# Two layers of a diffusion backbone on one core: latent tiles' norms placed behind the MLP's last squares, their transposes amid a projection, and a gate's store moved

## The chip, the cores and the metric

The kernel runs on one core of a Trainium2 chip. The time is device microseconds of one execution. An execution under the profiler gives the trace; its times count from the start of the span, which is the stretch between the first and the last instruction on the engines. In the rows, PE is the matrix engine (TensorE; PEld are its weight loads), DVE is VectorE, ACT is ScalarE, POOL is GpSimd and SP is the engine that issues DMAs (SPq its queue of issues).

## The reference, cut to what matters

512 latent tokens and 256 context tokens of 1024 channels go through two layers. Layer 0 mixes tokens by pooling, layer 1 by attention. Each sub-layer is normed before and after, modulated by vectors of a condition, and gated into a residual.

```python
for i in range(DEPTH):
    sh1, sc1, gt1, sh2, sc2, gt2 = ada_mods(c, w_ada[i], b_ada[i])
    h_lat = modulate(rms_norm(x, g_mix_pre[i]), sh1, sc1)
    h_ctx = modulate(rms_norm(ctx, g_mix_pre[i]), csh1, csc1)
    ...
    y_lat, y_ctx = attention_mixer(h_lat, h_ctx, w_qkv[j], g_q[j], g_k[j], w_o[j], not last)
    x = x + gt1 * rms_norm(y_lat, g_mix_post[i])
    m_lat = sq_relu_mlp(modulate(rms_norm(x, g_mlp_pre[i]), sh2, sc2), w_mlp_in[i], w_mlp_out[i])
    x = x + gt2 * rms_norm(m_lat, g_mlp_post[i])
```

## The kernel before

Tokens are handled in tiles of 128: tiles 0 to 3 are the latents, 4 and 5 the context. Every fp32 operand of a matmul is split into an upper and a lower part (hi and lo), and each product is three matmuls, so a projection of one tile by 512 columns is 24 matmuls (8 blocks of channels, three products each).

A scheduler, run when the program is built, orders each engine's instructions by its own estimate of time; the steps that the kernel records (`st.at(time, step, ...)`) give it their order of priority. `pin` and `tc.add_manual_dep(..., ISSUE)` fix the order of two instructions on one engine without a semaphore. What an engine then executes is a fixed list, each entry waiting for its semaphores; an entry that waits holds up all behind it on its engine.

The change touches two places.

The first is the passage from layer 0's MLP to layer 1's attention. `finish` takes the six tiles in the order 4, 5, 0, 1, 2, 3. For each it makes the last MLP product (`out_mm`: 24 matmuls into two banks called pso; for four of the tiles ACT first copies the earlier partial sum into the bank, a seed). Behind it come the steps of `last0` for this tile: `norm_a` squares the two halves on ACT (`junk<-pso`) and makes the post-norm's factor (its power is on POOL, `rs`), `norm_g` multiplies the sums by the gate on DVE (`work<-pso,gate`), which frees the banks, `norm_r` adds the result to the residual (`xl`, `xr`), `norm_s` squares the new residual on ACT (`junk<-xl`) for layer 1's norm, and `norm_c` scales the residual into `acc`. Two tiles together are then turned (`norm_pair`: 16 PE transposes into two psx buffers, eight modulations that ACT and DVE share, and the split into hi and lo parts, `ra`). At last `kv_a` projects one tile to keys and values (`project`, 24 matmuls into a psq bank), `kv_e`, `kv_b` and `kv_c` take the result on. Four banks (pool psB) serve pso, psq and pk in turn, and two double banks (psA) serve psx. The weights of the projection are split between the engines at the same time: three of the four lower parts of the second half are made on POOL (`units<-raw,units`).

The second place is the gate of attention's residual. It is 1024 numbers, made on DVE as a column of eight for each partition (`gate_cols`, tile gc), stored by a DMA to `grows` in DRAM (`gate_away`, issued on SP) and loaded back as one row for all partitions (`gate_back`). In the kernel before, `before0` calls `gate_away(1, GT1, 0)`, and the scheduler puts its product and its store in the midst of layer 0's MLP, amid loads of MLP weights that SP issues in order. The readers of the gate are the output steps of attention (`attn_ev`).

Of the kernel before, what the change touches and what calls it, by code (L numbers as in the profile page):

```python
# [17 lines left out]
P = 128  # L18
# [22 lines left out]
class Steps:  # L41
# [3 lines left out]
    def at(self, t, fn, *args):  # L45
        self.items.append((t, len(self.items), fn, args))
# [7 lines left out]
def backbone(ctx: ExitStack, tc, x, c, ctx_in, c_ctx, w_ada, b_ada, g_mix_pre, g_mix_post,  # L54
# [306 lines left out]
                      parts.rearrange("p (u c b a) -> p a u b c", c=nc_, b=2, a=4)[:, a], start=True, stop=True)  # L361
        ada_out(i, m, 0, ps[:, 0:2 * n], nc_, 8)

    def gate_cols(i, m, ci):
        gc = sm_tile("gc")
        g0 = (0 if m == GT1 else 16) + i * KT
        z = ve.tensor_tensor(out=gc, in0=mods[i][:, m * KT:(m + 1) * KT, ci], in1=gpc[:, g0:g0 + KT],
                         op=ALU.mult)
        pin(z, (i, m) == (0, GT1))
        if (i, m) == (1, GT2):  # L370
            tc.keep_in_program_order(z)
        return gc

    def gate_rows(i, m, ci):
# [8 lines left out]

    row_of = {(0, GT2, 0): 0, (0, GT2, 1): 1, (1, GT1, 0): 2, (1, GT2, 0): 3}

    def gate_away(i, m, ci):
        gc = gate_cols(i, m, ci)
        with nc.allow_non_contiguous_dma(reason="one column of gates for each partition"):
            sy.dma_start(rows_out[row_of[i, m, ci]].rearrange("(k p) -> p k", p=P), gc)

    def gate_back(i, m, ci):
        sy.dma_start(gate[:, ci, :], rows_out[row_of[i, m, ci]].partition_broadcast(P))

    def gate_half(h):
        gc = sm_tile("gc")
# [28 lines left out]
    def modulated_pair(t, i, s, hi, lo, works, wide, fine, on_act):  # L424
        if (i, s) == (0, 1):
            place = lambda z, ks: z.rearrange("p k (h q n) -> p k q h n", h=2, n=P)[:, ks, t // 2]
            split2 = lambda z: z.rearrange("p k (h n) -> p k h n", n=P)
        else:
            place, split2 = lambda z, ks: z[:, ks, slice(t * P, (t + 2) * P)], lambda z: z
        ci = 0 if t < NL else 1  # L430
        sh = (SH1, SH2)[s] * KT
        pss = []
        for q in range(4):
            if not wide:
                ps = psB.tile([P, 2, 256], F32, tag="b", name="psx")
            elif q % 2 == 0:
                both = psA.tile([P, 4, 256], F32, tag="a", name="psx")
            if wide:
                ps = both[:, 2 * (q % 2):2 * (q % 2) + 2, :]
            for kk in range(2):  # L440
                k = 2 * q + kk
                for u in range(2):
                    turned_[t] = te.transpose(ps[:, kk, u * P:(u + 1) * P], works[u][:, k * P:(k + 1) * P], ident)
            pss.append(ps)
        for q in range(4):
            h = works[q // 2][:, 512 * (q % 2):512 * (q % 2) + 512].rearrange("p (k n) -> p k n", n=256)
            for kk in range(2):
                k = 2 * q + kk
                sa, b = avec[i][s][:, k, ci:ci + 1], mods[i][:, sh + k, ci:ci + 1]
                if not on_act[k]:  # L450
                    ve.tensor_scalar(out=h[:, kk, :], in0=pss[q][:, kk, :], scalar1=sa, scalar2=b,
                                     op0=ALU.mult, op1=ALU.add)
                else:
                    sc.activation(h[:, kk, :], pss[q][:, kk, :], AF.Identity, scale=sa, bias=b)
            if fine:
                ks = slice(2 * q, 2 * q + 2)
                sc.copy(place(hi, ks), split2(h))
                ve.tensor_tensor(out=place(lo, ks), in0=split2(h), in1=place(hi, ks), op=ALU.subtract)
            elif q % 2:
                ks = slice(2 * q - 2, 2 * q + 2)  # L460
                h = works[q // 2].rearrange("p (k n) -> p k n", n=256)
                sc.copy(place(hi, ks), split2(h))
                if (i, s, q) == (1, 1, 3):
                    late.extend((place(lo, z), h[:, z.start - 4:z.stop - 4], place(hi, z)) for z in (slice(4, 6), slice(6, 8)))
                else:
                    ve.tensor_tensor(out=place(lo, ks), in0=split2(h), in1=place(hi, ks), op=ALU.subtract)
# [841 lines left out]

    b3 = lambda a: a.rearrange("p (h d) -> p h d", d=HD)

    def project(t, ws):
        ps = psB.tile([P, 512], F32, tag="b", name="psq")
        sl = slice(t * P, (t + 1) * P)
        for k in range(KT):
            wH, wL = ws[k // 4]
            for n, (a, w) in enumerate(((hH, wH), (hH, wL), (hL, wH))):
                te.matmul(ps, a[:, k, sl], w[:, k % 4, :], start=(k == 0 and n == 0),
                          stop=(k == KT - 1 and n == 2))
        return ps

    exps = {}
# [38 lines left out]
    pj = {}  # L1360
# [16 lines left out]
            gated(t, yg[t], src, c0, c0 + w, pool)  # L1377

    def kv_a(t):
        pj[t] = project(t, chunks[2])  # L1380

    def kv_e(t):
        ps = pj[t]
# [36 lines left out]
    def last0(st, n, t):  # L1420
        st.at([5.25, 10.45, 15.65, 20.85, 26.05, 27][n], norm_a, t)
        st.at([5.473, 10.6, 15.8, 21, 26.2, 27.1][n], norm_g, t, (False, False, False, False, False, False)[n])
        st.at([8.8, 14, 19.2, 24.4, 28.4, 30.3][n], norm_r, t, (False, True, False, False, False, False)[n])
        st.at([10, 16.738, 20.4, 25.6, 28.5, 30.4][n], norm_s, t, (False, False, False, False, True, False)[n])
        st.at([12, 17.906, 22.4, 27.6, 30.2, 30.6][n], norm_c, t, (True, True, True, True, True, False)[n], (False, False, False, False, False, False)[n])
        if t < NL:
            st.at([0, 0, 22.5, 27.7, 33, 37][n], lambda t: sy.dma_start(spill[:, t], xr[:, t]), t)
        if n % 2:
            st.at([18.2, 28.6, 39][n // 2], norm_pair, t - 1, 1, 0, hH, hL, True, (True, True, False)[n // 2],
                  ((True, False, False, False, False, False, False, True), (True, True, True, False, False, False, True, True), (True, False, True, False, True, False, True, False))[n // 2])  # L1430
        st.at([31.4, 36.6, 41.8, 47, 55, 60.2][n], kv_a, t)
        st.at([36.874, 40.793, 45.993, 51.193, 59.193, 65.4][n], kv_e, t)
        st.at([36.9, 42.1, 47.3, 52.5, 60.5, 65.7][n], kv_b, t)
        st.at([44.9, 50.1, 57.151, 62.351, 70.351, 75.551][n], kv_c, t)
        if t < NL:
            for ch in range(2):
                c = t + 4 * ch
                st.at([67.851, 73.051, 78.251, 81.6, 86.8, 92, 97.2, 104.478][c], q_a, ch, t)
                if c == 2 * NL - 1:
                    st.at(107.6, q_rest, ch, t)  # L1440
                st.at([71.2, 76.4, 81.6, 86.8, 92, 97.2, 102.4, 132][c], q_e, ch, t)
                st.at([71.5, 76.7, 81.9, 87.1, 92.3, 97.5, 102.7, 132.1][c], q_b, ch, t)
        if n == 5:
            st.at(18.4, rope_load)
            st.at(38.5, rope_tables)
            st.at(5.5, lambda: split(*raw0[0], True, False, True))
            raws = []
            st.at(31.3, w_chunk, 2, 1, raws)
            st.at(31.3, lambda: split(*raws[0], False, False, True, 0))
            st.at(31.301, lambda: split(*raws[0], False, False, True, 1))  # L1450
            st.at(31.302, lambda: split(*raws[0], False, False, True, 2))
            st.at(31.303, lambda: split(*raws[0], False, True, False, 3))
            st.at(52, w_chunk, 0, 0, raws)
            st.at(52.01, lambda: split(*raws[1], True, False, False))
            st.at(61, w_chunk, 0, 1, raws)
            st.at(61.01, lambda: split(*raws[2], True, False, False))
            st.at(61.1, w_chunk, 1, 0, raws)
            st.at(61.11, lambda: split(*raws[3], True, False, False))
            st.at(83, w_chunk, 1, 1, raws)
            st.at(83.01, lambda: split(*raws[4], True, False, False))  # L1460
            attention(st, 102.5, 2.7)
            output(st, 102.5 + 2.7 * 43.691)

    def before0():
        nonlocal xr, gate, junk
        for u in due:
            ada_fin(*u[1:])
        gate_away(1, GT1, 0)
        small.tile([P, 2, KT], F32R, tag="gh", name="phase2", bufs=2)
        S["held"].close()  # L1470
        xr, gate, junk = residents(held[1])
        gate_back(0, GT2, 1)
        gate_back(0, GT2, 0)
        for t in (4, 5, 0, 1, 2, 3):
            sy.dma_start(xr[:, t], spill[:, t])
        qring.append(Ring([unit[0], unit[2], unit[1]]))
        w_chunk(2, 0, raw0)
# [132 lines left out]
    def attention(st, base, unit_t):  # L1610
# [25 lines left out]
        at(39.192, lambda: split(*raws[3], False, False, False, 1))  # L1636
        at(39.193, lambda: split(*raws[3], False, False, False, 2))
        at(45.691, lambda: split(*raws[3], False, False, False, 3))
        at(36.95, gate_back, 1, GT1, 0)

    def output(st, base):
        at = lambda i, fn, *args: st.at(base + i, fn, *args)
# [95 lines left out]
```

## Time and profile before

| what | value |
|---|---|
| median of the runs | 1154.8 us (1154.6 to 1156.63, 3 runs) |
| the profiled execution itself | 1153.73 us |
| its span | 1151.9 us |
| mean granted clock of PE | 0.999 |
| loads of MLP input weights | 32, of 1 MB each |

Two ways to read the trace serve here. A timeline gives rows of "start, duration, engine, line, operation, output<-inputs, count", where a number in brackets is the idle time of the engine just before the row, and who ended it; equal instructions that follow each other are one row. A table of stretches gives, for each, the busy time of PE, PEld, DVE, ACT and POOL (with counts of instructions), the granted clock, the mean busy share of the DMA engines and the GB/s that they moved. Nearly all instructions have line 68, that of a helper, so rows are told apart by their tiles.

### The profile page before, as it was taken

To read this page: it belongs to the slowest core of one execution; us is meant where nothing else is said; L and a number is where in the kernel's file an instruction comes from. 1 tells how busy PE (TensorE), PEld (TensorE's weight loads), DVE (VectorE), ACT (ScalarE), POOL (GpSimd) and SP (SyncE) were. 2 spreads that over 40 slices of the span, in tenths; PEclk is the share of its full clock that TensorE was granted. 3 is DMA by queue.
4 is the path that set the end of the run, shared out by engine and by line. 5 is a ranking of instruction groups with operands and counts; after the bars stand their busy time and mean duration, and the time that the engine had idled before them with its cause. 6 is when DMAs were issued, how large, how long until landed. Compare 5 with 4: busy or idle time off the path is not lost.

```text
span 1151.9 us, 15610 instructions
## 1 busy us (share of the span) xinstructions
PE 1129.6 (98%) x5998; PEld 975.8 (85%) x5998; DVE 925.5 (80%) x1539; ACT 641.0 (56%) x1142; POOL 75.3 (7%) x82
## 2 busy tenths in 40 slices
PE   6999999999999999999999999999999999999998
PEld 5579889998888888989878889988988888888886
DVE  5798488889979999897577689977887779778875
ACT  6476655554335534555795468863876436435534
POOL 3040000000000000000241212100000000000000
PEclk9999999999999999999999999999999999999999
DMA  9992233244434434444652200046244224224303
GB/s 352 400 390 104 74 110 110 83 137 147 147 110 147 146 120 145 138 135 144 228 171 93 90 1 19 10 144 221 84 146 147 77 70 146 78 69 147 110 16 149
DMA packets 100042, 154.20 MB, mean 134 GB/s; under 512 B 7120, under 2 KB 72448, under 8 KB 99968
## 3 DMA queue, kind: packets, MB, share of 16 engines
q1 hardware_dynamic: 99872, 153.19, 38.5%
q8 instruction: 47, 0.77, 0.3%
q14 instruction: 27, 0.22, 0.1%
q10 hardware_dynamic: 96, 0.02, 0.0%
HBM read 143.75 MB, written 9.45 MB: 133 GB/s over the span
## 4 chain that ended last, share of the span: by engine, by line
PE 85%; ACT 5%; DVE 5%; DMA 3%; issue 1%; SPq 0%; POOL 0%; DVEq 0%; ACTq 0%
PE psin L68 32%; PE pso L68 30%; PE psq L68 7%; PE psy L68 4%; PE po L68 3%; PE pss L68 3%; DMA raw<-in_w_mlp_in 2%; PE pspt L68 1%; PE psada L68 1%; ACT junk L68 1%; PE pspool L68 1%; DVE acc L68 1%; DVE rows L68 1%; PE psx L68 1%; DMA raw<-in_w_ada 1%; ACT ra L68 1%
## 5 line engine op out<-in xcount | busy, mean ns | idle before, releaser
L68 PE MATMUL pso<-units,rb 128*128 128x512 f32 x1152 | 278.0, 392 | 0.0
L68 PEld LDWEIGHTS pso<-units,rb 128*128 128x128 f32 x1152 | 214.7, 188 | 42.0 <-ACT pso L68 0.7
L68 DVE TENSOR_TENSOR acc<-acc,pso 128x512 f32<-128x512 f32 x192 | 128.2, 681 | 62.2 <-PE pso L68 62.1
L68 DVE SCALAR_TENSOR_TENSOR rows<-raw,cond,rows 128x256 f32<-128x256 f32 x280 | 121.9, 478 | 0.9
L68 PE MATMUL psin<-ra 128*128 128x512 f32 (+1 forms) x424 | 112.3, 369 | 0.6 <-ACT work L68 0.6
L68 PE MATMUL psin<-ra,rb 128*128 128x512 f32 (+1 forms) x384 | 101.6, 360 | 0.1
L68 DVE TENSOR_TENSOR units<-raw,units 128x1024 fp32r<-128x1024 f32 (+2 forms) x69 | 82.9, 1212 | 16.2 <-ACT units L68 15.3
L68 ACT CAST units<-raw 128x1024 fp32r<-128x1024 f32 (+2 forms) x71 | 70.9, 1020 | 43.2 <-PE pso L68 19.6
L68 PE MATMUL psin<-rb,ra 128*128 128x384 f32 (+1 forms) x324 | 90.6, 356 | 0.0
L68 PEld LDWEIGHTS psin<-ra 128*128 128x128 f32 x424 | 77.9, 188 | 12.1 <-ACT work L68 1.0
L68 PE MATMUL psin<-ra,units 128*128 128x384 f32 x432 | 82.6, 336 | 0.0
L68 PE MATMUL pso<-units,pairs 128*128 128x512 f32 x336 | 82.3, 389 | 0.0
L68 ACT ACTIVATE work<-psin 128x512 f32<-128x512 f32 (+3 forms) x66 | 36.1, 552 | 82.0 <-PE psin L68 79.6
L68 PEld LDWEIGHTS psin<-ra,units 128*128 128x128 f32 x432 | 76.5, 188 | 2.8
L68 PEld LDWEIGHTS psin<-ra,rb 128*128 128x128 f32 x384 | 66.7, 189 | 11.6 <-issue 0.9
L68 PEld LDWEIGHTS pso<-units,pairs 128*128 128x128 f32 x336 | 63.1, 188 | 13.1
L68 PE MATMUL psin<-sums,units 128*128 128x384 f32 x336 | 63.9, 337 | 0.8 <-ACT psin L68 0.8
L68 PEld LDWEIGHTS psin<-rb,ra 128*128 128x128 f32 x324 | 58.6, 188 | 5.5
L68 PEld LDWEIGHTS psin<-sums,units 128*128 128x128 f32 x336 | 59.0, 188 | 2.4 <-ACT psin L68 1.2
L68 ACT COPY acc<-pso 128x512 f32<-128x512 f32 x68 | 38.5, 592 | 40.1 <-PE pso L68 39.9
L68 ACT ACTIVATE work<-work 128x768 f32<-128x768 f32 (+1 forms) x50 | 41.4, 831 | 32.2 <-DVE work L68 31.7
L68 ACT CAST rb<-raw 128x2048 fp32r<-128x2048 f32 (+2 forms) x18 | 25.8, 1432 | 58.9 <-PE pso L68 55.9
(221 smaller groups left out, 2093.1 us busy)
## 6 DMA issues: line engine op xcount, KB each, us to landing
raw<-in_w_ada SPq DMA_DIRECT2D x48, 1024.0 KB, 5.5
raw<-in_w_mlp_in SPq DMA_DIRECT2D x32, 1024.0 KB, 5.3
raw<-in_w_mlp_out SPq DMA_DIRECT2D x32, 1024.0 KB, 5.7
raw<-in_w_qkv SPq DMA_DIRECT2D x6, 1024.0 KB, 5.1
spill<-xl SPq DMA_DIRECT2D x8, 512.0 KB, 8.9
xl<-spill SPq DMA_DIRECT2D x8, 512.0 KB, 10.4
raw<-in_w_o SPq DMA_DIRECT2D x4, 1024.0 KB, 5.1
xl<-in_x SPq DMA_DIRECT2D x4, 512.0 KB, 5.6
```

The costliest lines, as they stand in the source:

```text
L68: z = made(*args, **kw)
```

## The change

Three edits, and what they do to each engine's list.

1. In `last0`, the steps `norm_s` and `norm_c` of the third and fourth tile (n = 2 and 3, which are latent tiles 0 and 1) get later times: 20.4 and 25.6 become 26.1 and 26.2, and `norm_c` of tile 0 goes from 22.4 to 26.15.
2. `kv_a` of context tile 5 gives `project` an instruction to stand behind: its matmuls for channel blocks 4 to 7 follow the last transpose of the pair of latent tiles 0 and 1.
3. `gate_away(1, GT1, 0)` moves from `before0` to a step of attention (time 3.3), with its product behind DVE's last modulation of latent pair 0; `gate_back(1, GT1, 0)` stands behind the copy of attention's ninth turn (`turned[8]`).

```diff
+        if behind is not None:
+            tc.add_manual_dep(z.ins, behind.ins.name, ISSUE, reason="row order")
         return gc
...
-    def gate_away(i, m, ci):
-        gc = gate_cols(i, m, ci)
+    def gate_away(i, m, ci, behind=None):
+        gc = gate_cols(i, m, ci, behind)
...
-    def gate_back(i, m, ci):
-        sy.dma_start(gate[:, ci, :], rows_out[row_of[i, m, ci]].partition_broadcast(P))
+    def gate_back(i, m, ci, behind=None):
+        z = sy.dma_start(gate[:, ci, :], rows_out[row_of[i, m, ci]].partition_broadcast(P))
+        if behind is not None:
+            tc.add_manual_dep(z.ins, behind.ins.name, ISSUE, reason="row order")
...
-                    ve.tensor_scalar(out=h[:, kk, :], in0=pss[q][:, kk, :], scalar1=sa, scalar2=b,
-                                     op0=ALU.mult, op1=ALU.add)
+                    turned_[t, ve] = ve.tensor_scalar(out=h[:, kk, :], in0=pss[q][:, kk, :], scalar1=sa, scalar2=b,
+                                                      op0=ALU.mult, op1=ALU.add)
...
-    def project(t, ws):
+    def project(t, ws, behind=None):
...
-                te.matmul(ps, a[:, k, sl], w[:, k % 4, :], start=(k == 0 and n == 0),
+                z = te.matmul(ps, a[:, k, sl], w[:, k % 4, :], start=(k == 0 and n == 0),
                           stop=(k == KT - 1 and n == 2))
+                if behind and k >= 4:
+                    tc.add_manual_dep(z.ins, behind.ins.name, ISSUE, reason="row order")
...
-        pj[t] = project(t, chunks[2])
+        pj[t] = project(t, chunks[2], turned_[0] if t == NL + 1 else None)
...
-        st.at([10, 16.738, 20.4, 25.6, 28.5, 30.4][n], norm_s, t, (False, False, False, False, True, False)[n])
-        st.at([12, 17.906, 22.4, 27.6, 30.2, 30.6][n], norm_c, t, (True, True, True, True, True, False)[n], (False, False, False, False, False, False)[n])
+        st.at([10, 16.738, 26.1, 26.2, 28.5, 30.4][n], norm_s, t, (False, False, False, False, True, False)[n])
+        st.at([12, 17.906, 26.15, 27.6, 30.2, 30.6][n], norm_c, t, (True, True, True, True, True, False)[n], (False, False, False, False, False, False)[n])
...
-        gate_away(1, GT1, 0)
...
-        at(36.95, gate_back, 1, GT1, 0)
+        at(3.3, lambda: gate_away(1, GT1, 0, turned_[0, ve]))
+        at(36.95, lambda: gate_back(1, GT1, 0, turned[8]))
```

On PE, from the turn of the context pair to the projections of latent tiles (pso are the last MLP products, psx the turns, psq the projections):

```order
 L68 MATMUL psx<-ident,acc 128x128 x14
 L68 MATMUL pso<-units,rb 128x512 x32
-L68 MATMUL psx<-ident,acc 128x128 x2
+L68 MATMUL psq<-rb,ra 128x512 x19
+L68 MATMUL psq<-units,ra 128x512 x4
+L68 MATMUL psq<-rb,ra 128x512 x5
+L68 MATMUL psq<-units,ra 128x512 x8
+L68 MATMUL psx<-ident,acc 128x128 x16
+L68 MATMUL psq<-units,ra 128x512 x12
+L68 MATMUL psx<-ident,acc 128x128 x16
 L68 MATMUL psq<-rb,ra 128x512 x12
 L68 MATMUL psq<-units,ra 128x512 x12
```

Before, two transposes of latent pair 0 stood right behind the MLP, then 31 projection matmuls and the other 14; the second pair was turned in two halves with projection matmuls between them. Now 36 projection matmuls come first, then the first pair as a whole, 12 matmuls of context tile 5, and the second pair as a whole.

On ACT, the list from the square of tile 5's new residual (`junk<-xr`) on. Before (5030 belongs to tile 0's residual, pso 4947 and 4948 are tile 1's sums, 5081 and 5082 tile 3's banks):

```order
L68 ACTIVATE junk_4816,ss_4985<-xr_4814 128x1024
L68 ACTIVATE ss_4985<-ss_4985,phase_112 128x1
L68 ACTIVATE junk_4816,ss_5030<-xl_4820 128x1024
L68 ACTIVATE acc_93<-xr_4814,rs_4988 128x1024
L68 ACTIVATE ss_5030<-ss_5030,phase_112 128x1
L68 ACTIVATE junk_4816,ss_5063<-pso_4947 128x512
L68 ACTIVATE ss_5063<-ss_5063,phase_112 128x1
L68 ACTIVATE junk_4816,ss_5063<-pso_4948 128x512
L68 ACTIVATE acc_93<-xl_4820,rs_5033 128x1024
L68 ACTIVATE acc_93<-psx_4991,mods1_100,avec10_103 128x256
```

And in the changed kernel (pso 4944 and 4945 are tile 1's sums, 5067 and 5068 tile 3's banks, 5027 tile 2's first sum):

```order
L68 ACTIVATE junk_4813,ss_4982<-xr_4811 128x1024
L68 ACTIVATE ss_4982<-ss_4982,phase_112 128x1
L68 ACTIVATE junk_4813,ss_5055<-pso_4944 128x512
L68 ACTIVATE ss_5055<-ss_5055,phase_112 128x1
L68 ACTIVATE junk_4813,ss_5055<-pso_4945 128x512
L68 ACTIVATE acc_93<-xr_4811,rs_4985 128x1024
L68 COPY pso_5067<-acc_93 128x512
L68 ACTIVATE ss_5055<-ss_5055 128x1
L68 COPY pso_5068<-acc_93 128x512
L68 ACTIVATE acc_93<-psx_4988,mods1_100,avec10_103 128x256
L68 ACTIVATE junk_4813,ss_5095<-pso_5027 128x512
```

Tile 0's residual square and scaling (`junk<-xl`, `acc<-xl`) have left this place; the square stands seven rows behind the last one shown, the scaling behind all squares of tile 3's sums. Tile 1's squares now come ahead of tile 5's scaling (`acc<-xr`), the seeds of tile 3 ahead of the modulations, and tile 2's first squares right behind the first modulation.

On SP, in layer 0's MLP (grows<-gc is the gate's store):

```order
 L147 DMA raw<-in_w_mlp_out 128x2x1024
-L389 DMA grows<-gc 128x8x1
 L147 DMA raw<-in_w_mlp_in 128x8x256
 L147 DMA raw<-in_w_ada 128x8x256 x2
```

and later on SP, in attention (gate<-grows is the load of the gate, spill and in_w_qkv and in_w_o are the residual's stores and the weights):

```order
 L147 DMA raw<-in_w_qkv 128x4x512
-L392 DMA gate<-grows 128x1024
-L1427 DMA spill<-xl 128x1024 x2
+L1433 DMA spill<-xl 128x1024
+L391 DMA grows<-gc 128x8x1
 L147 DMA raw<-in_w_qkv 128x4x512
 L147 DMA raw<-in_w_o 128x4x512 x4
-L1608 DMA acc<-spill 128x1024
+L394 DMA gate<-grows 128x1024
+L1613 DMA acc<-spill 128x1024
```

The store has left its place between two loads of MLP weights and now stands ahead of a load of projection weights; the load of the gate stands behind the last load of `w_o`.

More of the change, by code (lines that the diff above doesn't have):

```diff
@@ L362, in ada_fin, with gate_cols @@
         ada_out(i, m, 0, ps[:, 0:2 * n], nc_, 8)
-    def gate_cols(i, m, ci):
+    def gate_cols(i, m, ci, behind=None):
         gc = sm_tile("gc")
```

## The prediction

> **What bounds the kernel now.** First the page's totals, then the table of stretches, to see where TensorE (PE) is not full.
>
> ```profile
> span 1151.9 us, 15610 instructions
> PE 1129.6 (98%) x5998; PEld 975.8 (85%) x5998; DVE 925.5 (80%) x1539; ACT 641.0 (56%) x1142; POOL 75.3 (7%) x82
> 580.00:600.00 20.00, 18.59 (x90) 15.09 (x89) 16.36 (x23) 17.81 (x45) 10.93 (x10) 1.00 0.60 197
> ```
>
> PE is busy for 98% of the span, so no edit that leaves PE's instructions alone can bring more than the gaps between them. The change adds and removes none of PE's 5998. The stretch 580 to 600, in which the change reorders PE, misses 1.41 us. So I look for that gap, in PE's timeline and in that of its weight loads (PEld).
>
> ```profile
> 579.61 7.73 PE L68 MATMUL pso<-units,rb 128*128 128x512 f32 x32
> 587.17 0.38 PE L68 MATMUL psx<-ident,acc 128*128 128x128 f32 x2
> 588.97 3.02 PE L68 MATMUL psq<-rb,ra 128*128 128x512 f32 x12 [1.41 <-DVE work L68]
> ...
> 601.99 1.03 PE L68 MATMUL psx<-ident,acc 128*128 128x128 f32 x8
> 602.78 1.17 PE L68 MATMUL psq<-rb,ra 128*128 128x512 f32 x4
> ```
>
> ```profile
> 577.95 1.66 PEld L68 LDWEIGHTS psx<-ident,acc 128*128 128x128 f32 x14
> 581.59 5.32 PEld L68 LDWEIGHTS pso<-units,rb 128*128 128x128 f32 x24 [0.33 <-ACT pso L68]
> ```
>
> The last matmuls of layer 0 end at 587.5, and the first projection of layer 1 (psq) starts 1.41 late. A smaller wait of 0.33 stands at 581.59, for a seed that ScalarE (ACT) copies into a bank. The chain of waits says who is behind the large one.
>
> ```profile
> 587.61 0.58 ACT junk L68 x2
> 588.22 0.70 DVE work L68
> ```
>
> ACT squares latent tile 2's sums, VectorE (DVE) then multiplies them by the gate, which frees the bank, and PE goes on at 588.97. ACT was the late one:
>
> ```profile
> 575.73 1.04 ACT L68 ACTIVATE junk<-xl 128x1024 bf16<-128x1024 f32 x1
> ...
> 576.77 1.14 ACT L68 ACTIVATE acc<-xr,rs 128x1024 f32<-128x1024 f32 x1
> ...
> 577.99 0.57 ACT L68 ACTIVATE junk<-pso 128x512 bf16<-128x512 f32 x1
> ...
> 579.46 1.14 ACT L68 ACTIVATE acc<-xl,rs 128x1024 f32<-128x1024 f32 x1
> ...
> 591.68 1.15 ACT L68 ACTIVATE acc<-xl,rs 128x1024 f32<-128x1024 f32 x1 [0.78 <-POOL rs L68]
> 594.26 0.63 ACT L68 ACTIVATE junk<-xl 128x512 bf16<-128x512 f32 x1 [1.25 <-DVE xl L68]
> ...
> 598.68 0.26 ACT L68 ACTIVATE junk<-psq 128x128 bf16<-128x128 f32 x1
> ...
> 598.94 1.47 ACT L68 ACTIVATE acc<-psx,mods,avec 128x256 f32<-128x256 f32 x3
> ...
> 600.54 1.16 ACT L68 CAST ra<-acc 128x512 fp32r<-128x512 f32 x2
> 601.57 1.05 ACT L68 ACTIVATE acc<-psx,mods,avec 128x256 f32<-128x256 f32 x2
> ```
>
> From 575.73 to 598.94 ACT idles only 0.78 + 1.25 = 2.03 us (the rows between name no other wait). PE and ACT are thus both nearly full here. That is the key to this change: making PE earlier helps only as far as ACT can follow.
>
> **Term 1, the projection's start.** ACT now does latent tile 2's squares, and the seeds for tile 3, ahead of the residual squares and the scaling of tiles 0 and 1. The waits of 1.41 and 0.33 should go: -1.74 us. Tile 2's squares then wait only for PE itself, some 6 us before 587.5.
>
> **Term 2, context tile 5's turn.** Before, ACT had tile 0's square (575.73 to 576.77: 1.04) ahead of the scaling of tile 5 (576.77), on which the turn at 577.95 rests. Now two halves of tile 1's squares stand there, which take 577.99 to 579.46, 1.47 us. The scaling is 0.43 later. It ended at 576.77 + 1.14 = 577.91, and PEld's turn row starts at 577.95: no slack. So +0.43.
>
> **Term 3, the latents' turns.** PE's time from here: 579.61 + 0.43, then 32 matmuls at (587.17 - 579.61 - 0.33) / 32 = 0.226 us: the projection starts at 587.3. The 36 projection matmuls now ahead of the first turn take 8.1 (to 595.4), 16 turns at (602.78 - 601.99) / 8 = 0.10 take 1.6 (597.0), the 12 other matmuls of context tile 5 take 2.7: PE wants the turn of tiles 2 and 3 at about 599.7. Before, it began at 601.99. The turn needs the buffer of the first pair to be emptied by three modulations on ACT and one on DVE, and tile 3 to be scaled.
>
> ACT's work ahead of the first of these is the same set as before, less one head square (0.26, the row at 598.68), so it is 575.73 plus 598.94 - 0.26 - 575.73 - 2.03 = 20.9 us plus the new idle times. I count two. First, tile 2's first sum is complete at 580.0 + 5 x 0.226 + a tail of 0.2 = 581.4, and ACT stands in front of it from about 580.0 (tile 5's scaling ends at 578.3, and two seed copies, a small step and a modulation of about 0.5 each follow): 1.4 idle. Second, tile 0's scaling waits for a power on GpSimd (POOL), behind three splits of weights:
>
> ```profile
> 584.37 4.48 POOL L68 TENSOR_TENSOR units<-raw,units 128x512 fp32r<-128x512 f32 x2 [1.98 <-ACT units L68]
> 588.80 0.61 POOL L68 CAST units<-raw 128x512 fp32r<-128x512 f32 x1
> 589.38 1.31 POOL L68 TENSOR_TENSOR units<-raw,units 128x512 fp32r<-128x512 f32 x1
> 590.64 1.52 POOL L68 TENSOR_TENSOR rs<-ss,nhalf 128x1 f32<-128x1 f32 x2
> ```
>
> POOL now does one split (half of 4.48, 2.24), a power (half of 1.52, 0.7), the cast (0.6), two splits (2.24 and 1.31) and then tile 0's power (0.7), from about 584.5, when ACT has made the first split's upper part: 592.3. ACT is there at about 591.6 (an estimate: 20 pieces from 581.4 on, each as long as the same piece was before, 10.2 in all), so 0.7 idle. The first modulation falls at 575.73 + 20.9 + 2.1 = 598.7, three end at 600.1, DVE's one at about 600.7, and PE has waited 1.0 (DVE's small product for the gate comes ahead of tile 3's scaling, which waits for POOL longer than that). The second half of the turn needs two more modulations behind a head square and a cast (0.4 with its readout, then 0.5 and 0.9 by the rows at 600.54 and 601.57: to 601.9) against PE's 600.7 + 8 x 0.1 = 601.5: 0.4 more. Term 3: +1.4. Bounds: nothing if ACT's idle times vanish; 2.9 if each of them is 0.75 longer. The value is near the middle because both idle times are built from rows.
>
> The sum of terms 1 to 3 is +0.1, between -1.3 and +1.6. Later stages of the attention layer keep their order and hang on PE, so nothing hides it.
>
> **Term 4, the gate's store leaves layer 0.** The two issues and their landings, then the DMA columns (share, GB/s) of two stretches:
>
> ```profile
> L389 SPq DMA_DIRECT2D grows<-gc x1: 462/462/462, 324.1 to 324.1; - x1
> DMA to landing us min/median/max: 13.4/13.4/13.4
> ...
> L147 SPq DMA_DIRECT2D raw<-in_w_mlp_in x1: 368/368/368, 333.1 to 333.1; - x1
> ...
> DMA to landing us min/median/max: 8.7/8.7/8.7
> ...
> raw<-in_w_mlp_in SPq DMA_DIRECT2D x32, 1024.0 KB, 5.3
> ```
>
> ```profile
> 334.00:336.00 2.00, 2.00 (x12) 1.83 (x11) 0.69 (x1) 0.21 (x1) 0.00 (x0) 1.00 0.19 4
> ...
> 338.00:340.00 2.00, 2.00 (x11) 1.62 (x10) 1.12 (x3) 0.00 (x0) 0.00 (x0) 1.00 1.03 330
> ```
>
> The 4 KB store lands at 324.1 + 13.4 = 337.5. The weights issued at 333.1 move at 4 GB/s until then and at 330 right after, and land in 8.7 instead of 5.3 us. What follows:
>
> ```profile
> 341.84 1.05 ACT L68 CAST units<-raw 128x1024 fp32r<-128x1024 f32 x1 [5.46 <-DMA raw<-in_w_mlp_in]
> 343.95 1.22 PEld L68 LDWEIGHTS pso<-units,rb 128*128 128x128 f32 x6 [0.33 <-ACT pso L68]
> 353.46 2.35 PE L68 MATMUL psin<-sums,units 128*128 128x384 f32 x12 [0.77 <-ACT psin L68]
> ```
>
> (three views: ACT's, PEld's and PE's timelines). ACT waits for the load, and PE for ACT, twice: 0.33 + 0.77 = 1.1 us. Without the store the load should land 3.4 us earlier, more than both waits: -1.1. The bounds are 0 (another cause keeps the load late) and -1.1. I take -1.1, since the bandwidth rises within 2 us of the store's landing. The Trainium skill, "DMA: Bandwidth & Descriptors", section "Queues, rings and completion order", says that on each DMA engine one issuer's descriptors are consumed in ring order; by that rule the large load stood behind the store's small pieces, the rows agree, and the store would hold up whatever is queued behind it in its new place too.
>
> **What I cost at nothing.** Rows of SP's timeline, of the page's DMA issues and of the gate's tile:
>
> ```profile
> 621.24 0.38 SPq L147 DMA_DIRECT2D raw<-in_w_qkv  x1
> ...
> gate<-grows SPq DMA_DIRECT2D x4, 512.0 KB, 6.6
> ...
> L68 DVE TENSOR_TENSOR acc<-psy,gate x9: 404/691/692, 772.7 to 813.6; 128x512 f32<-128x512 f32 x7, 128x256 f32<-128x256 f32 x2
> ```
>
> The store's new issue is at about 599, behind a spill and ahead of a load that SP issued at 621.24; the store has landed by 612.5, so that load covers it, and without that cover it would cost up to 13.4 - 5.3 = 8 us of a load's landing. The reload of the gate moves from 593 to behind attention's ninth turn, near 700, with the reloads of the residual queued behind it on SP, whose readers come behind 772.7 too; the gate's first reader is at 772.7, which leaves some 70 us for a landing of 6.6. The small product on DVE leaves 323.5, where DVE is not late.
>
> **Sum.** +0.1 - 1.1 = -1.0 us on the profiled execution's own 1153.73 us (its span is 1151.9), which is 1.07 below the median of the runs shown. Against 1154.8 that makes 1153.8 us.
>
> **Rivals.** (a) The turns are in time: ACT's new idle times do not come, since tile 1's and tile 2's squares fill them. Terms 1, 2 and 4 remain: -2.4, 1152.4 us. For it speaks that ACT's work is not more; against it that PE's own order keeps tile 2's sum open until 581.4. (b) It turns slower: POOL's splits run against DVE's subtractions.
>
> ```profile
> L68 DVE TENSOR_TENSOR ra<-acc,ra x4: 680/681/1802, 584.1 to 585.9; 128x512 fp32r<-128x512 f32 x4
> ```
>
> One of four equal subtractions took 1.80 instead of 0.68 beside POOL's split: 1.1 lost. Now two splits run later, beside a residual and more subtractions, and ahead of the powers of tiles 0, 1 and 3. Two such losses on the way to the modulations are 2.2: -1.0 + 2.2 = +1.2, 1156.0 us. It decides for slower from the point where tile 0's power ends 1.0 later than my 592.3. The Trainium skill, "SBUF — State Buffer", section "SBUF: two separate sides", states that a GpSimd operation and a VectorE operation with two SBUF inputs exclude each other for a whole instruction; the 1802 ns row agrees, and by that rule each overlap costs the full 1.1 on one of the two, which is this rival's time. (c) The store is not what delays the load: term 4 is 0, 1154.9 us.
>
> **Chances and range.** Forecast 0.55, (a) 0.20, (b) 0.13, (c) 0.12. With the measurement's own spread I put the range from 1152.0 to 1156.0, which takes in (a) and (b). A measurement of this kernel tells some 0.2% (2.3 us) from no change. Only (a), with a little more, passes below 1152.5: 0.16 faster. Only the far end of (b) passes 1157.1: 0.05 slower. So 0.79 for the same.
>
> **What would show it.** In the changed profile: psq follows pso with no wait near 587; PEld's turn of tile 5 waits about 0.4; PE waits some 1 us for ACT or DVE at the turn of tiles 2 and 3, near 600; no wait at 344 and 353, and the load issued at 333 lands in about 5.3 us. A full PE from 588 to 605 means (a); a POOL power for tile 0 past 593.3 means (b); a load that still takes 8 us means (c). A PE wait in attention or behind 620 would make the whole reading wrong.

## The result, and the profile after

| | before | changed |
|---|---|---|
| median of 20 runs each, same chip | 1154.72 us (1154.04 to 1156.63) | 1152.78 us (1152.28 to 1154.08) |
| ratio, 95% interval | | 0.9982 [0.9975, 0.9989] |
| the profiled execution, its span | 1153.73, 1151.9 us | 1152.6, 1150.8 us |

The medians differ by 1.94 us, the two profiled executions by 1.13 us. That these two numbers are not the same is half of what follows. First the page of the changed kernel (span; busy time, share and count of each engine):

```profile
span 1150.8 us, 15601 instructions
PE 1129.7 (98%) x5998; PEld 976.6 (85%) x5998; DVE 925.9 (80%) x1539; ACT 640.0 (56%) x1142; POOL 76.0 (7%) x82
```

PE's work is the same to 0.1 us. What was won are gaps, and to see where, I compare the starts of equal matmuls in PE's timeline of both kernels. The changed kernel:

```profile
341.47 2.27 PE L68 MATMUL psin<-ra 128*128 128x384 f32 x12
...
352.38 2.26 PE L68 MATMUL psin<-sums,units 128*128 128x384 f32 x12
...
359.80 2.24 PE L68 MATMUL psin<-rb,ra 128*128 128x384 f32 x12
...
575.15 0.38 PE L68 MATMUL psx<-ident,acc 128*128 128x128 f32 x2
...
577.22 1.75 PE L68 MATMUL psx<-ident,acc 128*128 128x128 f32 x14
578.72 7.53 PE L68 MATMUL pso<-units,rb 128*128 128x512 f32 x32
586.09 4.47 PE L68 MATMUL psq<-rb,ra 128*128 128x512 f32 x19
...
599.99 2.20 PE L68 MATMUL psx<-ident,acc 128*128 128x128 f32 x16 [1.08 <-DVE acc L68]
...
613.37 3.02 PE L68 MATMUL psq<-rb,ra 128*128 128x512 f32 x12
```

And the four of before that mark the ends of the two places:

```profile
341.32 2.27 PE L68 MATMUL psin<-ra 128*128 128x384 f32 x12
...
360.97 2.24 PE L68 MATMUL psin<-rb,ra 128*128 128x384 f32 x12
...
576.32 0.38 PE L68 MATMUL psx<-ident,acc 128*128 128x128 f32 x2
...
614.58 3.02 PE L68 MATMUL psq<-rb,ra 128*128 128x512 f32 x12
```

The place in layer 0, from the first of these rows to the second, took 360.97 - 341.32 = 19.65 us and takes 18.33: 1.32 less. From there to the two turns at 576 it is 215.35 in both. The passage between the layers, from the turns to latent tile 2's projection, took 614.58 - 576.32 = 38.26 and takes 38.22. So the whole gain of this pair of profiles is made in layer 0, and the two edits of the passage cancel. The load of layer 0, seen by the DMAs of its line, lands in 5.2 us where it took 8.7, and the wait of 0.77 at 353 is gone (that row now starts at 352.38):

```profile
L147 SPq DMA_DIRECT2D raw<-in_w_mlp_in x1: 367/367/367, 333.7 to 333.7; - x1
...
DMA to landing us min/median/max: 5.2/5.2/5.2
```

In the passage the projection now follows the MLP with no wait (586.09), and a new wait of 1.08 stands at the turn of latent tiles 2 and 3. The timelines of PEld and ACT there, in this order:

```profile
577.21 1.51 PEld L68 LDWEIGHTS psx<-ident,acc 128*128 128x128 f32 x14 [0.50 <-ACT acc L68]
...
599.99 0.85 PEld L68 LDWEIGHTS psx<-ident,acc 128*128 128x128 f32 x8 [1.50 <-DVE acc L68]
601.10 0.86 PEld L68 LDWEIGHTS psx<-ident,acc 128*128 128x128 f32 x8 [0.25 <-ACT acc L68]
```

```profile
580.16 0.60 ACT L68 ACTIVATE junk<-pso 128x512 bf16<-128x512 f32 x1 [1.31 <-PE pso L68]
...
591.54 1.15 ACT L68 ACTIVATE acc<-xl,rs 128x1024 f32<-128x1024 f32 x1 [1.39 <-POOL rs L68]
...
597.90 1.46 ACT L68 ACTIVATE acc<-psx,mods,avec 128x256 f32<-128x256 f32 x3
```

This is an exchange of waits: ACT took tile 2's squares first, which freed the bank in time, and so it idles in front of tile 2's first sum (1.31) and of a power behind POOL's splits (1.39), and the modulations that the turn needs begin at 597.90.

### The profile page after: what moved, and what is told of

Read it like the earlier page. It is cut to its first block, busy times and chain, and to the rows that moved or that the text cites. A ratio compares the mean times of both kernels' runs of the same rounds, so it can differ in the third digit from the quotient of the medians.

```text
span 1150.8 us, 15601 instructions
## 1 busy us (share of the span) xinstructions
PE 1129.7 (98%) x5998; PEld 976.6 (85%) x5998; DVE 925.9 (80%) x1539; ACT 640.0 (56%) x1142; POOL 76.0 (7%) x82
## 3 DMA queue, kind: packets, MB, share of 16 engines
q1 hardware_dynamic: 99872, 153.19, 39.2%
## 5 line engine op out<-in xcount | busy, mean ns | idle before, releaser
L68 DVE TENSOR_TENSOR units<-raw,units 128x1024 fp32r<-128x1024 f32 (+2 forms) x69 | 83.1, 1214 | 15.9 <-ACT units L68 15.8
L68 PEld LDWEIGHTS psin<-ra 128*128 128x128 f32 x424 | 77.8, 188 | 12.1 <-ACT work L68 1.0
```

The lines of the kernel that those rows point to most:

```text
L68: z = made(*args, **kw)
```

## Experiments

The first two take the change apart, the third doubles what the first one moves.

**Only the store's DMA moved.** All the rest is the kernel before; the four compute engines keep their order.

```diff
-        gate_away(1, GT1, 0)
+        early_gc.append(gate_cols(1, GT1, 0))
...
+            z = sy.dma_start(rows_out[2].rearrange("(k p) -> p k", p=P), early_gc[0])
+        tc.add_manual_dep(z.ins, turned[0].ins.name, ISSUE, reason="row order")
...
+        at(3.3, store_late)
```

> Before, with one DMA moved: the store of attention's gate (4 KB) is issued by SP behind the last load of w_o instead of amid layer 0's MLP; the lists of all four compute engines are the same as before. Theory T (the store holds up the weight load queued behind it): that load lands in 5.2 to 5.4 us instead of 8.7, PE's waits of 0.33 and 0.77 us near 344 and 353 are gone, the wait of 1.41 near 588 stays, and the time is 1.1 to 1.9 us below before (ratio 0.9984 to 0.9990). Rival S (the gain comes from the order of the compute engines): the load may land earlier, but the time stays within 0.3 us of before.

Measured: 1152.95 us (1152.68 to 1153.21), ratio 0.9986 [0.9978, 0.9995]; the before of these runs 1154.8. The load lands in 5.5 us, and the place in layer 0 takes 18.32 us. So moving one DMA issue makes the change's whole gain, as far as the intervals tell (the ratio of the whole change, 0.9982, lies inside this one's).

**Everything but the store's move.**

```diff
+        gate_away(1, GT1, 0)
...
-        at(3.3, lambda: gate_away(1, GT1, 0, turned_[0, ve]))
-        at(36.95, lambda: gate_back(1, GT1, 0, turned[8]))
+        at(36.95, gate_back, 1, GT1, 0)
```

> The changed kernel with its third edit undone: norms and turns as changed, the gate's store and load where they were before. Theory T with balanced terms in the passage between the layers: PE's wait of 1.41 near 588 is gone, waits of about 0.5, 1.1 and 0.25 stand at the turns near 577, 600 and 601, the load in layer 0 still lands in 8 to 9 us, and the time is within 0.4 us of before. Rival S (the new order is the gain): 1.1 to 1.9 us below before.

Measured: 1154.79 us (1153.99 to 1155.56), ratio 1.0002 [0.9994, 1.0011]. The passage takes the same 38.26 us as before, although its waits stand elsewhere: the edits to the norms, turns and projections move work and bring nothing that can be told.

**The store twice.** The kernel before, with a second copy of the store, to an unused row, right behind the first.

```diff
+            if (i, m) == (1, GT1):
+                sy.dma_start(rows_out[4].rearrange("(k p) -> p k", p=P), gc)
```

> Before, with the gate's store issued twice in a row in layer 0 (the second to an unused row of the DRAM buffer); nothing else moves. Theory T: the weight load behind them starts to move only when the second store has landed, some 10 to 13 us later than before, so it lands in 15 to 22 us instead of 8.7, and PE waits some 8 to 13 us more near 350: 1163 to 1168 us. Rival S, or stores that run beside each other on the queue: the load lands in about 9 us, and the time stays within 0.5 us of before.

Measured: 1163.98 us (1161.48 to 1164.29), ratio 1.0077 [1.0065, 1.009]: 9 us slower for 4 KB more. The load lands in 15.9 us, and PE waits for it:

```profile
341.26 2.27 PE L68 MATMUL psin<-ra 128*128 128x384 f32 x12
350.55 1.01 PE L68 MATMUL psin<-ra,units 128*128 128x384 f32 x2 [7.02 <-ACT units L68]
```

The stretches of this run (the last two columns are the DMA engines' share and GB/s) show how:

```profile
340.00:342.00 2.00, 2.00 (x12) 1.77 (x11) 0.00 (x0) 0.00 (x0) 0.00 (x0) 1.00 0.84 36
...
346.00:348.00 2.00, 0.00 (x0) 0.00 (x0) 0.00 (x0) 0.00 (x0) 0.00 (x0) 1.00 0.84 217
```

The DMA engines are as busy at 36 GB/s as at 217. The load does not stand still behind the second store; it crawls, at 22 to 46 GB/s, until that store has landed at 325.05 + 21.3 = 346.4.

Is it the number of pieces, or the queue? The next two ask that.

**The store in 128 pieces.** The kernel before, with the row written in the order of partitions, 32 bytes a piece in place of 4. The reloaded gate has its columns permuted, so attention's residual is gated by the wrong columns. The work is the same: the turns stand at 574.88 and the span is 1150.8 us, against 574.89 and 1151.0 with only the DMA moved.

```diff
-            sy.dma_start(rows_out[row_of[i, m, ci]].rearrange("(k p) -> p k", p=P), gc)
+            sy.dma_start(rows_out[row_of[i, m, ci]].rearrange("(p k) -> p k" if (i, m) == (1, GT1) else "(k p) -> p k", p=P), gc)
```

> The kernel before, in which the gate's store of layer 0 stays where it is but writes its row in the order of partitions: 128 pieces of 32 bytes in place of 1024 of 4 (so the gate of attention, reloaded from it, has its columns permuted). If the number of small pieces makes the store slow and so the load behind it late (P), the store lands in under 5 us, the load issued at 333 lands in 5.2 to 5.5 us, the waits of PE at 344 and 353 go, and the median is that of the run with the store alone moved: 1152.7 to 1153.3. If any store ahead of the load on SP delays it, whatever its pieces (Q), nothing changes: 1154.4 to 1155.2.

Measured: 1152.64 us (1152.43 to 1153.02), ratio 0.9982 [0.9973, 0.999], a little below the range that was expected. The landings of the three stores up to 330, then that of the load behind the last of them:

```profile
DMA to landing us min/median/max: 4.7/13.4/14.3
...
DMA to landing us min/median/max: 5.4/5.4/5.4
```

The two other stores, still of 1024 pieces, land in 13.4 and 14.3 us, this one in 4.7, with the same bytes from the same place. The page of this run counts 98976 packets on SP's queue where before has 99872, which is 896 or 1024 - 128 fewer. So the way the store is cut up is the cause (P). Number, size and spacing of the pieces changed together, and which of them counts isn't shown. To win the time the store doesn't have to move; but a correct kernel would also have to put the columns back in order, which wasn't tried.

**The store from ACT's queue.**

```diff
-            sy.dma_start(rows_out[row_of[i, m, ci]].rearrange("(k p) -> p k", p=P), gc)
+            (sc if (i, m) == (1, GT1) else sy).dma_start(rows_out[row_of[i, m, ci]].rearrange("(k p) -> p k", p=P), gc)
```

> The kernel before, with the gate's store of layer 0 issued by ACT in place of SP, at the same point of the program. If the load is late because it stands behind the store in SP's own queue (P), it now lands in 5.2 to 5.5 us, and the median is 1152.7 to 1153.3 (0.2 more if ACT's issue of some 0.5 us delays its next copies). If the store's pieces take the DMA engines themselves, whoever issues them (Q), the load still lands in 7.5 to 9 us and the median stays at 1154.4 to 1155.2.

Measured: 1153.96 us (1152.98 to 1156.14), ratio 0.9995 [0.9986, 1.0004]. The store still takes 12.1 us, the load 7.3:

```profile
336.00:338.00 2.00, 2.00 (x12) 1.86 (x12) 0.51 (x3) 0.59 (x1) 0.00 (x0) 1.00 0.83 193
```

Time and landing lie between the two forecasts, so by the numbers neither holds. The rows speak for the second (Q). The store was issued at 324.22 and landed at 336.3, the load at 333.56, landing at 340.9: 4.5 us behind the store. In the kernel before the load landed at 341.8, 4.3 us behind the store's 337.5. So the load came sooner here in step with the store, which was done 1.2 us sooner; the 193 GB/s (58 before in the same stretch) fall nearly all behind the store's landing. Ahead of it the load crawls here too:

```profile
334.00:336.00 2.00, 2.00 (x11) 1.79 (x10) 0.68 (x1) 0.00 (x0) 0.00 (x0) 1.00 0.20 7
```

That is 7 GB/s, against 4 in the kernel before. The Trainium skill, "DMA: Bandwidth & Descriptors", section "Queues, rings and completion order", says that SP and ACT own separate rings on the same 16 engines, which serve them in turn. This pair can't show that: by the same view as the next one, the store's pieces have passed the engines by 329.0, before the load starts.

Nor did the load stand behind the store's pieces at the DMA engines. Here are the kernel before from 326 to 334 (the engines' busy tenths in 40 slices of 0.2 us, the packets, and the queue of instruction loads), one of its stretches, and the same queue with the store in 128 pieces:

```profile
DMA  9999899999971000000000009000000000000000
DMA packets 1245, 0.79 MB, mean 99 GB/s; under 512 B 1056, under 2 KB 1056, under 8 KB 1244
q8 instruction: 1, 0.02, 2.3%
...
332.00:334.00 2.00, 2.00 (x11) 1.70 (x11) 1.05 (x3) 0.00 (x0) 0.00 (x0) 1.00 0.00 0
...
q8 instruction: 1, 0.02, 0.8%
```

All the small packets (the 1024 pieces and 32 others) have passed the engines in the first 13 slices, by 328.6. From there the engines are idle but for one load of 16 KB of instructions. The weights' load, issued at 333.11, thus met idle engines, and still crawled until the store landed at 337.5. The load of instructions, on a queue of its own, was slowed as well: it took 2.9 us (2.3% of 16 engines' 8 us) with the store of 1024 pieces out, 2.7 with that store on ACT's queue, and 1.0 with 128 pieces. So it isn't a place in a ring that slows the load. A load that starts when such a store's pieces have passed but the store hasn't landed is slow, on SP's queue or on that of the instructions, with the store on SP's queue or on ACT's. What the store still has to do between 328.6 and 337.5 isn't shown by any view.

**How far the hold-up varies.** The kernel before twice more, unchanged, for a second and a third profile.

> The kernel before once more, for a second profile. Its runs spread over 4 us (1152.4 to 1156.6), those with the store moved over 0.6. If the time that the store holds up the load differs from execution to execution (P), this profile shows another landing than 8.7 us for the load issued at 333, with waits of PE at 344 and 353 that differ from 1.1 us in sum by about as much as the span differs from 1151.9. If the spread comes from elsewhere (Q), landing and waits are the same and the span differs by what another stretch shows.

> The kernel before, a third profile, to see how far the load's landing (8.7 and 9.0 us in the two so far) and its time go together. If the hold-up varies by execution (P), this execution's time is 1153.7 to 1156, and above 1153.73 by about as much as PE's waits between 340 and 360 are above those of the first profile. If it is not (Q), the waits are the same and the time differs elsewhere.

Measured: 1154.17 us with a landing of 9.0, and 1156.75 us with a landing of 10.4. PE's timeline in the third:

```profile
341.67 2.27 PE L68 MATMUL psin<-ra 128*128 128x384 f32 x12
345.51 0.62 PE L68 MATMUL psin<-ra,units 128*128 128x384 f32 x2 [1.57 <-ACT units L68]
346.52 2.64 PE L68 MATMUL pso<-units,rb 128*128 128x512 f32 x6 [0.39 <-ACT pso L68]
...
364.06 2.24 PE L68 MATMUL psin<-rb,ra 128*128 128x384 f32 x12
...
579.38 0.38 PE L68 MATMUL psx<-ident,acc 128*128 128x128 f32 x2
```

The place takes 364.06 - 341.67 = 22.39 us here; from its end to the turns it is 215.32, as ever. The wait costs more than itself here, for the granted clock (third column from the right) falls to a half behind it:

```profile
346.00:347.00 1.00, 0.61 (x3) 0.44 (x3) 1.00 (x2) 1.00 (x2) 0.00 (x0) 0.94 0.00 0
347.00:348.00 1.00, 1.00 (x4) 0.81 (x3) 1.00 (x3) 0.97 (x2) 0.00 (x0) 0.50 0.00 0
...
350.00:351.00 1.00, 1.00 (x6) 0.96 (x5) 1.00 (x2) 0.97 (x3) 0.00 (x0) 0.86 0.00 0
```

Landings and times moved as the theory of the hold-up (P) has it, but neither forecast came as it was put. In the second profile PE's two waits are 0.38 and 0.76, 1.14 us where the first has 0.33 + 0.77 = 1.10, and the span is 0.5 longer: what grew is PEld's waits, from 0.33 + 1.20 to 0.34 + 0.70 + 1.19. The third is above the range of 1153.7 to 1156, and its waits of PE (1.57 + 0.39) give only 0.86 of the 3.02 us by which it is slower than the first; the clock adds 1.7. What holds in all three is the time of the whole place.

All the profiles in one table. "Lands" is the load's landing, counted from the start of PE's first row (the one at 341), "place" the time between the two rows of layer 0:

| execution | load takes | lands | place | its own time |
|---|---|---|---|---|
| changed kernel | 5.2 | -2.6 | 18.33 | 1152.6 |
| only the DMA moved | 5.5 | -2.7 | 18.32 | 1152.75 |
| 128 pieces | 5.4 | -2.2 | 18.32 | 1152.57 |
| from ACT's queue | 7.3 | -0.7 | 18.43 | 1152.99 |
| before, first | 8.7 | +0.5 | 19.65 | 1153.73 |
| all but the store's move | 8.6 | +0.8 | 20.02 | 1153.99 |
| before, second | 9.0 | +1.1 | 20.31 | 1154.17 |
| before, third | 10.4 | +2.7 | 22.39 | 1156.75 |
| store twice | 15.9 | +8.2 | 27.96 | 1162.46 |

A load that lands 2.2 us ahead of the row or earlier costs nothing, and one that lands 0.7 ahead costs 0.1; from there on each us of lateness costs about one, and some more where the clock falls. The three executions of before differ from the changed one by 1.13, 1.57 and 4.15 us. The place gives 1.32, 1.98 and 4.06 of it, and where the first row starts (341.32, 341.02 and 341.67 against 341.47) the rest, -0.15, -0.45 and +0.20, to within about 0.1 us. So these executions differ because the store's hold-up does (P). For the runs without a profile that is argued from the spread: runs with the store ahead of the load in layer 0 have standard deviations of 0.5 to 1.1 us, those without 0.16 to 0.37.

The last two kernels ask whether the passage has something left.

**Tile 0's square two steps earlier.** The changed kernel, with ACT's square of latent tile 0 taken earlier.

```diff
-        st.at([10, 16.738, 26.1, 26.2, 28.5, 30.4][n], norm_s, ...)
+        st.at([10, 16.738, 24, 26.2, 28.5, 30.4][n], norm_s, ...)
```

> The changed kernel with one number altered: the square of latent tile 0's new residual is recorded at 24 instead of 26.1, which puts it on ACT between the two seeds of tile 3, where ACT idled 1.31 us in front of tile 2's first sum; the scaling of tile 0 follows some ten pieces earlier, and two transposes of the first latent pair stand ahead of the projection. If ACT's work ahead of the latents' modulations is what PE waits for near 600 (1.08 + 0.25 us in the changed kernel), those waits shrink to 0 to 0.3 and the time falls by 0.8 to 1.3 us below the changed kernel (1151.5 to 1152.0). If instead POOL's splits decide (ACT waits 1.39 us for tile 0's power), the power comes ahead of the splits and the gain is the same or more; if PE now waits at the two early transposes, the gain is lost: within 0.3 us of the changed kernel.

Measured: 1152.77 us (1152.37 to 1152.95), ratio 0.9983 [0.9974, 0.9992], the same as the changed kernel. Of what was expected, PE's waits near 600 did shrink, to one of 0.61, and no wait came at the two early transposes; the gain was lost elsewhere. The passage became shorter, 612.73 - 574.93 = 37.80 us where it was 38.22, but most of it was lost again at the turn of latent tile 3's keys, here PE's, DVE's and ACT's timelines in this order:

```profile
635.76 0.41 PE L68 MATMUL pk<-ident,xr 128*128 128x128 f32 x2 [0.21 <-DVE xr L68]
```

```profile
634.60 0.69 DVE L68 TENSOR_TENSOR lent<-raw,lent 128x512 fp32r<-128x512 f32 x1
635.20 0.42 DVE L68 TENSOR_TENSOR xr<-work 128x256 f32<-128x256 f32 x1
```

```profile
631.39 1.67 ACT L68 CAST lent<-raw 128x512 fp32r<-128x512 f32 x3 [0.80 <-DMA raw<-in_w_o]
```

DVE makes xr behind its splits of w_o, whose upper parts ACT makes when the load has landed: at 631.39 here, at 631.51 in the changed kernel (a wait of 0.29 there). PE came 0.64 earlier, the load 0.12. The load is the next bound, some 20 us behind the end of the passage.

**One of POOL's splits on DVE.** The changed kernel, with one of the two splits that POOL makes ahead of tile 0's power given to DVE.

```diff
-            st.at(31.302, lambda: split(*raws[0], False, False, True, 2))
+            st.at(31.302, lambda: split(*raws[0], False, False, False, 2))
```

> The changed kernel, in which VectorE takes one of the two weight splits that GpSimd has at 586.6 (each about 2 us there, about 0.7 on VectorE). If tile 0's power behind GpSimd's splits makes ACT's scaling late and so the turn of tiles 2 and 3 (T), ACT's idle of 1.39 at 591.5 shrinks to under 0.5, one of VectorE's two subtractions of 1.8 us beside the splits goes back to 0.7, and PE's wait of 1.08 at 600 goes to under 0.4. The span then falls by at most 0.3, since the loads of w_o land at 631.4 as they did with tile 0's scaling moved, and the median stays at 1152.3 to 1152.9. If ACT's own work sets the turn (R), the wait at 600 stays at 0.8 to 1.2 and ACT idles elsewhere before it.

Measured: 1152.46 us (1152.27 to 1153.18), ratio 0.9983 [0.9974, 0.9992] against a before of 1154.4. ACT's idle time for POOL went from 1.39 to 0.92, not below 0.5, and the modulations began 0.73 earlier (597.17), but PE's wait stayed, in two parts, 0.97 in sum:

```profile
599.26 0.33 PE L68 MATMUL psx<-ident,acc 128*128 128x128 f32 x1 [0.28 <-DVE acc L68]
600.28 1.85 PE L68 MATMUL psx<-ident,acc 128*128 128x128 f32 x15 [0.69 <-DVE acc L68]
```

```profile
598.52 0.29 ACT L68 ACTIVATE ss<-ss,phase 128x1 f32<-128x1 f32 x1
...
598.88 0.55 POOL L68 TENSOR_TENSOR rs<-ss,nhalf 128x1 f32<-128x1 f32 x1 [3.30 <-ACT ss L68]
...
599.47 0.75 DVE L68 TENSOR_SCALAR acc<-xl,rs 128x1024 f32<-128x1024 f32 x1 [0.26 <-POOL rs L68]
```

(rows of three engines: ACT, POOL, DVE.) The scheduler, given other estimates, put ACT's small step for tile 3's power behind the three modulations instead of ahead of them, and tile 3's scaling became the late one. So POOL does set when the modulations begin (T), but without it the turn waits for tile 3 (nearer R). Whether the wait would go with tile 3's step in its old place wasn't tried.

## Why the prediction was right, and where its sum was off

**Term 1** (the waits of 1.41 and 0.33 go) was right: the prediction had the projection at 587.3 on the clock of before, and less the 1.17 by which the turns at 576 start earlier that is 586.1; it starts at 586.09.

**Term 2** (+0.43 at tile 5's turn): PEld waits 0.50 there. On PE it is less, 578.72 - 575.15 = 3.57 against 579.61 - 576.32 = 3.29, so +0.28.

**Term 3** (+1.4): PE waits 1.08 and PEld 1.50 and 0.25, where 1.0 and 0.4 were expected. ACT's two idle times came, 1.31 and 1.39 against 1.4 and 0.7. The second was longer because ACT was there sooner than my estimate, at 590.15 (591.54 - 1.39) where I had 591.6 - 1.2 = 590.4, and POOL was later, at 591.5 where I had 592.3 - 1.2 = 591.1. The first modulation began at 597.90, 0.4 later than the 598.7 - 1.2 that I had.

Terms 1 to 3 together are 38.22 - 38.26 = -0.04 us by the profiles, with +0.1 predicted, and the kernel without the store's move shows nothing by its median either.

**Term 4** (the store leaves layer 0) had the right mechanism and the wrong size. Its -1.1 was the sum of two waits of PE in one profiled execution. In that execution the place gave 1.32; PEld's waits there are 0.33 and 1.20, of which the second shows on PE as 0.77. But for the median it is nearly twice as much: the run with the DMA alone moved gives 1154.8 - 1152.95 = 1.85 us (0.6 to 2.5 by its interval), the one with 128 pieces 1154.74 - 1152.64 = 2.1 us (1.2 to 3.1). The step that failed is the one that carried the sum from the profiled execution to the median, as if the 1.07 us between them were a constant. Most likely they were lateness of this very load in executions that the profile did not show; in the changed kernel the profiled execution lies only 0.2 below its median. The bounds of term 4, 0 and -1.1, were those of one execution as well. That this stands for the median rests on the table's three executions of before and on the spreads; the landing in a median execution wasn't seen by itself.

One reason given for term 4 was wrong. The prediction had the load standing behind the store's pieces in ring order and said that the rows agree. They don't: the pieces had passed the DMA engines by 328.6, and from ACT's queue the store held up SP's load as well. Nor did the load move at 4 GB/s all the way to 337.5; from 336 to 338 it had 58. That the store's landing frees the load was right, and the term rested on that.

The time came out inside the range because the far end of rival (a) had been taken in, not because that rival came: (a) said that the turns would be in time, and they wait 1.08. **Rival (b)**, POOL against DVE, came in its first half only. DVE's and POOL's timelines of the changed kernel, in this order:

```profile
587.59 1.78 DVE L68 TENSOR_TENSOR units<-raw,units 128x512 fp32r<-128x512 f32 x1
589.30 1.79 DVE L68 TENSOR_TENSOR ra<-acc,ra 128x512 fp32r<-128x512 f32 x1
```

```profile
586.56 3.98 POOL L68 TENSOR_TENSOR units<-raw,units 128x512 fp32r<-128x512 f32 x2
590.50 2.04 POOL L68 TENSOR_TENSOR rs<-ss,nhalf 128x1 f32<-128x1 f32 x3
```

Two subtractions of DVE took 1.1 us longer beside POOL's splits, just as the rival had it. But DVE was not on the way to the modulations then, and ACT's scaling of tile 0 began at 591.54, ahead of the 593.3 - 1.2 = 592.1 from which the rival would have decided. The Trainium skill, "SBUF — State Buffer", section "SBUF: two separate sides", gives the exclusion for a whole instruction; the rows agree, and with one split taken from POOL one of the two subtractions went back to 0.7. **Rival (c)**, that the store isn't the cause, is out by three runs: moved, doubled, and cut into fewer pieces.

What I had **costed at nothing** stayed so. No landing is recorded for the store in its new place, issued at 598.23; with the 12.4 to 14.3 us of the others it is there by 612.5, before SP issues the load at 619.66, and that load takes 5.1 us (5.0 before). The gate's reload is issued at 650.55, not near 700, which leaves more room ahead of its first reader. No wait of PE appears behind 620 in the changed kernel that was not there before. Two more stores of 1024 pieces stay in every kernel, at 292; the weights issued behind them at 304 take 6.6 to 7.3 us, and PE doesn't wait for them.

## What to carry to other kernels

Look at small stores by their pieces, not their bytes: 4 KB in 1024 pieces held up the 1 MB load behind it by 3.5 us or more, and the same 4 KB in 128 pieces by nothing; move such a store to where nothing urgent is loaded until it has landed, or shape it. Giving it to another issuer is no cure: from ACT's queue 0.8 of some 2 us was won, within the noise. When runs of a kernel spread more than its variants do, profile it several times: a wait that one profile shows as 0.77 us may be where the spread is made, and the term should be sized by the spread, not by the one execution. And where two engines are both full in a passage, expect reordering to exchange waits; ask which load or split, here 20 us later, is the next bound before counting a gain.

## What the runs showed of the hardware that I had not expected

- The hold-up is not a matter of the queue. The store's pieces had passed the DMA engines 4.5 us before the load was issued, the engines were idle in between, and the load still crawled until the store's landing; from either queue it landed 4.3 to 5.2 us behind it. With two stores ahead, it moved at 22 to 46 GB/s until the second had landed. In the prediction I had argued from order alone.
- The store, issued at 324.07, 324.14 and 324.98, took 13.4, 13.3 and 14.2 us in the three executions of before, and the load behind it 8.7, 9.0 and 10.4. The second and the third ran on different chips, but runs of before on one chip spread too, by 1.8 to 4.2 us. What makes the difference stays open.
- In the third execution of before, PE's waits of 1.57 and 0.39 us were followed by about 3.4 us at half the granted clock (0.50 between 347 and 350, with parts of the stretches on either side, which costs 1.7 us of work), while in all three the wait of 1.41 at the projection was followed by none. The Trainium skill, "TensorE: Matmul & The Clock Gate", section "What's actually happening", gives a window of about 3.4 us that runs freely; the length of the slow stretch agrees, but the wait ahead of it was less than half a window long. In the run with the store twice, the wait of 7.02 us was followed by about 6.8 at half the clock.
